# A two-layer RG-LRU and mLSTM trunk: a gate projection in seven half products, another product order, square roots in one block, and half of an output quarter moved

## The chip, the cores and the metric

The kernel runs as one program on one core of one Trainium2 chip. The metric is the device time of one execution in microseconds (us), the median of the runs shown. All matrix work is done by TensorE (PE in the profile, with its weight loads listed as PEld). VectorE (DVE), ScalarE (ACT) and GpSimd (POOL) do the rest, and SyncE (SP) issues the plain loads and stores.

## The reference

The input is x with 512 tokens of 1024 channels, in float32. Each of two layers computes, with h the modulated RMS norm of x:

```
u = h @ w_in[l]
rg_x, rg_z, ml_x, ml_o, ml_z = jnp.split(u, split_pts, axis=-1)
y_rg = rglru(causal_depthwise_conv(rg_x, ...), ...) * jax.nn.silu(rg_z)
y_ml = mlstm_branch(ml_x, ml_o, ...) * jax.nn.silu(ml_z)
y = jnp.concatenate([y_rg, y_ml], axis=-1) @ w_out[l]
x = x + gate[:, None, :] * y
```

Each of the five pieces of u has 1024 columns. The RG-LRU needs, of each channel, r = sigmoid(block product + bias), a power exp(-8 r softplus(-lambda)), a factor sqrt(1 - a*a), and a scan over the tokens. The mLSTM has four heads of 256 channels, worked in the quadratic form over four blocks of 128 tokens.

## The kernel before, in words

**Precision.** A float32 product is made of three: each operand is split into a high part (a cast to fp32r on ACT) and a low part (the difference, on DVE), and `mm3` (L505 to L508) issues high x high, high x low and low x high into the same PSUM bank. All matmuls are recorded by `Planner.mm` and so stand at L154. A weight unit is 512 KB: `load_raw` fetches it to a tile of kind raw, and `split` makes whi (L184, ACT) and wlo (L191, DVE), so each unit costs one pass on each of the two engines. There are six raw tiles, four whi and four wlo.

**Order.** Nothing is issued as it is written. The kernel records operations; `Planner.deadlines` places each by the due time of the matmul that needs it, from costs written into the class; `Planner.schedule` runs a list schedule over PE, ACT, DVE, POOL and SP; and `issue` emits the instructions in that order. Every engine then works through its own list in order, and waits where an operand isn't there.

**A layer.** The ml_x projection (tiles mx), the four heads' scores (p, v, S), then the gates ml_o and ml_z (`ml_oz`, tiles oz) head by head with the heads' value products between (num, yT). Then the RG part: the rg_x projection (`rg_x`) and the rg_z projection (`rg_z`), each in four groups g of 256 columns, the gate products (`rg_gates`, tiles pa and px), and `rg_tail` for channel blocks 0 to 3 (batch 0) and 4 to 7 (batch 1). Then the output product in three column ranges: 512 columns (`out_first`, tiles out), 256 columns (`out_quarter`, tiles outq), 256 columns block by block of tokens (`out_last`, tiles outq as well). Every range sums the mLSTM's 1024 rows first (the list `CORD`), then the RG-LRU's.

**A group** (`chan_group`, L764) has two weight units, one for each half of the 1024 input channels, and 48 matmuls: 2 column halves x 8 input blocks x 3, each with a 128x128 weight block stationary and all 512 tokens moving.

**Seven products.** `ml_oz` makes the 512 tokens x 1024 x 512 columns of a head's two gates from seven half-size products instead of eight: tokens, input channels and columns are each cut in two. Four combinations of the h blocks (`h_forms`, tiles sf, sh, sl) are made once per layer; the combinations of weight quarters are made in the raw tile, by an accumulating DMA that POOL issues (`qdma`, L241: raw<-raw). One tile, ta, goes through four forms in turn: it is split, added to, split again. A product is 24 matmuls with 256 columns moving. In `ml_oz` the products come in the order h11, s1, s2, h12, s3, h22, s4; the two input halves are the even and the odd blocks of 128 channels.

**rg_gates** clamps r's argument on DVE (`q<-pa,par`, L208) ahead of an Exp. **rg_tail** takes the four square roots of a batch (`om<-om`) as four separate operations, and ACT's functions need a table that holds them (ACT_TABLE_LOAD).

**Background.** The next modulation's products are summed on DVE between the rest (`mod_units`, tiles macc), two steps for each `step_mod`, and finished by matmuls (modT, gateps) in the output stage.

Of the kernel before, what the change touches and what calls it, by code (L numbers as in the profile page):

```python
# [19 lines left out]
L = 2  # L20
D = 1024
T = 512
NB = 4
# [23 lines left out]
class View:  # L47
# [21 lines left out]
    def spread(self, axis, n):  # L69
        shape = list(self.dummy.shape)  # L70
        shape.insert(axis, n)
        d = np.broadcast_to(np.expand_dims(self.dummy, axis), shape)
        return self._next(d, lambda a: a.unsqueeze(axis).to_broadcast(shape))

# [34 lines left out]
class Planner:  # L109
# [55 lines left out]
    def act(self, out, in_, func, scale=None, bias=None, accum=None, extra=0.0):  # L165
        def r(v):
            return v.ap() if isinstance(v, View) else v

        def emit():
            kw = {}  # L170
            if scale is not None:
                kw["scale"] = r(scale)
            if bias is not None:
                kw["bias"] = r(bias)
            if accum is not None:
                kw["accum_out"] = accum.ap()
            self.nc.scalar.activation(out=out.ap(), in_=in_.ap(), func=func, **kw)
# [3 lines left out]
        self.op("ACT", emit, outs, [in_, scale, bias], 0.1 + 0.00084 * in_.n + 0.093 * k + extra)  # L181

# [254 lines left out]
def trunk_kernel(ctx: ExitStack, tc: tile.TileContext, x, cT, params, bif, bgate, fg,  # L437
# [6 lines left out]
    def pools(name, n, **kw):  # L444
# [3 lines left out]
        "heap": pools("heap", 64),  # L448
# [139 lines left out]
    sp4, hb = keep("sp4", [128, L, 8]), keep("hb", [128, L, 16])  # L588

    def small_params():  # L590
# [8 lines left out]
        P.ts(hb, par[:, :, P_BA:P_BA + 16], 0.5, ALU.mult)  # L599

# [395 lines left out]
    def ml_oz(l, h, hT, st):  # L996
# [3 lines left out]
        src = w_oz[l, h].rearrange("u p (k w n) -> p u k w n", k=2, w=2)  # L1000
        q = [src[:, :, k, w, :] for k in range(2) for w in range(2)]
        form = [[(hT[2 * p + k][0][:, ts], hT[2 * p + k][1][:, ts]) for p in range(4)]
                for k, ts in ((0, slice(0, 256)), (1, slice(0, 256)), (1, slice(256, 512)))]
        h11, h12, h22 = form
# [5 lines left out]
        def quarter(src):  # L1010
            raw = P.tile("raw", (128, 4, 256), F32, "raw")
            P.dma(raw, src, 1 << 19)
            return raw

        def add(raw, src):
            P.qdma(raw, src, 1 << 19)
# [10 lines left out]
        def wide(name):  # L1027
            return slot(name, F32, (128, 2, 256))

        ta = quarter(q[0])  # L1030
        ps = product(h11, parts(ta))
        p1 = wide("ozp")
        P.acopy(p1, ps)
        tb = quarter(q[1])
        add(ta, tb)
        p5 = product(s1, parts(ta))
        c12, c22 = wide("ozc"), wide("ozc")
        P.acopy(c22, p5)
        td = quarter(q[3])
        add(ta, td)  # L1040
        ps = product(s2, parts(ta))
        u = wide("ozu")
        P.tt(u, ps, p1, ALU.add)
        P.tt(c12, c22, u, ALU.subtract)
        tc = quarter(q[2])
        ps = product(h12, parts(tc))
        o = [wide("oz") for _ in range(2)]
        z = [wide("oz") for _ in range(2)]
        P.tt(p1, ps, p1, ALU.add)
        P.act(o[0], p1, AF.Tanh, scale=0.5)  # L1050
        yield
        add(tb, td)
        ps = product(s3, parts(tb))
        P.tt(u, ps, u, ALU.add)
        P.tt(c22, c22, u, ALU.subtract)
        add(ta, tc)
        ps = product(h22, parts(ta))
        P.tt(u, ps, u, ALU.add)
        P.act(o[1], u, AF.Tanh, scale=0.5)
        ps = product(s4, parts(td))  # L1060
        P.tt(c12, ps, c12, ALU.add)
        for n, c in ((1, c22), (0, c12)):
            P.act(z[n], c, AF.Tanh, scale=0.5)
            P.stt(z[n], z[n], 1.0, c, ALU.add, ALU.mult)
# [75 lines left out]

    def rg_x(l, g, hT, st):
# [10 lines left out]
    def rg_gates(l, g, st):  # L1152
# [4 lines left out]
        for cc in range(2):  # L1157
# [9 lines left out]
            P.ts(q, pa, par[:, l, P_BA + r:P_BA + r + 1], ALU.add, 0.0, ALU.min)  # L1167
            P.act(tr, pa, AF.Tanh, scale=0.5, bias=hb[:, l, r:r + 1])
            P.act(q, q, AF.Exp)
# [12 lines left out]
    def rg_z(l, g, hT, st):  # L1182
        pz = chan_group(l, 4 + g, hT, ("rgz0", "rgz1"))
# [19 lines left out]
    def out_evac(l, ps, xt, cs):  # L1203

        cw = cs.stop - cs.start
        t = slot("og", F32, (128, cw))
        P.tt(t, ps, gate_t[l][:, cs], ALU.mult)
# [17 lines left out]

    def out_quarter(l, st, xt, side):
        y = st["y"]
        ps = [bank("outq", (128, 256)) for b in range(NB)]
        for u in range(4):
            wh, wl = load_w(w_out[l, 8 + u], (4, 256))  # L1230
            for b in range(NB):
                bs = slice(128 * b, 128 * b + 128)
                for k in range(4):
                    c = CORD[4 * u + k]
                    mm3(ps[b], y[c][0][:, bs], y[c][1][:, bs], wh[:, k, :], wl[:, k, :], u == 0 and k == 0,
                        u == 3 and k == 3)
            side(u)
        for b in range(NB):
            out_evac(l, ps[b], xt[b], slice(512, 768))

    def out_last(l, st, xt, units, b):
# [3 lines left out]
        for u, (wh, wl) in enumerate(units):  # L1245
            for k in range(4):
                c = CORD[4 * u + k]
                mm3(ps, y[c][0][:, bs], y[c][1][:, bs], wh[:, k, :], wl[:, k, :], u == 0 and k == 0, u == 3 and k == 3)
        out_evac(l, ps, xt[b], slice(768, 1024))
# [37 lines left out]
    for l in range(L):  # L1287
        st = {k: {} for k in ("xm", "xc", "S", "v", "oz", "sw", "y", "yt", "A", "xr", "ai", "rz", "gq", "gv")}
# [98 lines left out]
        rg_z(l, 3, hT, st)  # L1387
# [23 lines left out]
        units = [load_w(w_out[l, 12 + u], (4, 256)) for u in range(4)]  # L1411
# [85 lines left out]
```

## Time and profile before

| what | value |
|---|---|
| median of 3 runs | 827.79 us (827.75 to 828.91) |
| the profiled execution, its own time | 827.94 us |
| its span, first to last instruction | 826.0 us, so 1.9 us lie around the span |
| granted TensorE clock, mean | 0.999 |
| RG part of layer 0 on PE | 226.3 to 330.9 us |
| RG part of layer 1 on PE | 624.0 to 728.6 us |

Times inside the profile are us from the start of the span. A row of the chain of waits reads: start, length, engine, tile and line, and xN for so many instructions in a row. A row of the groups of instructions reads: line, engine, operation, out<-in, shapes, xcount | busy us, mean ns of one | idle time of the engine ahead of them. Matmuls overlap, so the mean length of one (280 or 390 ns) is not the distance from one to the next; the chain's pieces give that distance. On DVE and ACT as well an instruction starts a little before the one ahead of it has ended. A row of the windows holds, for each engine, busy us and the number of instructions, then the granted clock, the DMA share and GB/s.

### The profile page before, as it was taken

The page shows a single profiled execution, that of the slowest core. Times are in us where ns is not written, and L with a number is a line of the kernel's source. Part 1 is how long each engine was busy: PE and PEld are TensorE (multiplying, and loading weights), DVE is VectorE, ACT ScalarE, POOL GpSimd, SP SyncE. Part 2 cuts the span into 40 slices and gives each one's busy share as a digit, 9 for nine tenths or more (in the row PEclk, how much of TensorE's full clock was granted, in tenths as well). Part 3 has the DMA queues.
Part 4 walks back from the last instruction along what each step waited for, and adds up shares of the span by engine and source line. Part 5 has one row for each costly group of instructions (what it writes and reads, how often), then busy time and mean ns, then how long its engine had stood idle before and what let it go on. Part 6 is the DMA issues. An engine that isn't in the chain of part 4 may idle for free.

```text
span 826.0 us, 14051 instructions
## 1 busy us (share of the span) xinstructions
PE 807.3 (98%) x5222; PEld 718.8 (87%) x5222; DVE 676.5 (82%) x1339; ACT 536.2 (65%) x1049; POOL 66.0 (8%) x96
## 2 busy tenths in 40 slices
PE   4999999999999999999999999999999999999996
PEld 3778899999988888889999789999998888888996
DVE  4678976899999899989469886589999989995552
ACT  4468765687858979822148666648786797992221
POOL 3000012122100000000010001212210000000000
PEclk9999999999999999999999999999999999999999
DMA  8953255668533434787433434368753243483002
GB/s 302 336 216 111 71 126 131 126 155 203 154 102 127 154 112 161 253 293 263 181 99 102 150 92 87 52 160 198 182 130 124 102 157 104 150 312 120 26 1 102
DMA packets 53956, 124.46 MB, mean 151 GB/s; under 512 B 4865, under 2 KB 23297, under 8 KB 53889
## 3 DMA queue, kind: packets, MB, share of 16 engines
q1 hardware_dynamic: 49280, 106.80, 38.2%
q0 software_dynamic: 4608, 16.78, 11.5%
q8 instruction: 41, 0.67, 0.3%
q14 instruction: 27, 0.21, 0.1%
HBM read 102.58 MB, written 4.19 MB: 129 GB/s over the span
## 4 chain that ended last, share of the span: by engine, by line
PE 96%; ACT 1%; DMA 1%; DVE 1%; issue 0%; SPq 0%; POOLq 0%; ACTq 0%
PE oz L154 18%; PE mx L154 11%; PE outq L154 11%; PE rgx L154 11%; PE out L154 11%; PE rgz L154 11%; PE S L154 4%; PE num L154 3%; PE v L154 3%; PE p L154 3%; PE A L154 2%; PE px L154 1%; PE pa L154 1%; DMA x<-in_x_dram 1%; PE hT L163 1%; PE modps L154 1%
## 5 line engine op out<-in xcount | busy, mean ns | idle before, releaser
L184 ACT CAST whi<-raw 128x1024 fp32r<-128x1024 f32 (+1 forms) x157 | 156.4, 1003 | 112.1 <-PE out L154 32.5
L191 DVE TENSOR_TENSOR wlo<-raw,whi 128x1024 fp32r<-128x1024 f32 (+1 forms) x157 | 180.7, 1158 | 39.6 <-ACT whi L184 38.9
L154 PE MATMUL oz<-whi,sh 128*128 128x256 f32 x256 | 72.8, 284 | 0.0
L154 PE MATMUL oz<-whi,sl 128*128 128x256 f32 x256 | 72.3, 283 | 0.0
L154 PE MATMUL oz<-wlo,sh 128*128 128x256 f32 x256 | 72.1, 282 | 0.0
L154 PE MATMUL outq<-whi,yh 128*128 128x256 f32 x256 | 71.5, 283 | 0.0
L154 PE MATMUL outq<-whi,yl 128*128 128x256 f32 x256 | 71.3, 282 | 0.0
L154 PE MATMUL outq<-wlo,yh 128*128 128x256 f32 x256 | 71.2, 282 | 0.0
L154 PE MATMUL mx<-hh,whi 128*128 128x512 f32 (+1 forms) x166 | 59.5, 358 | 2.2 <-ACT whi L184 2.2
L154 PE MATMUL mx<-hl,whi 128*128 128x512 f32 (+1 forms) x166 | 58.1, 350 | 0.1
L154 PE MATMUL mx<-hh,wlo 128*128 128x512 f32 (+1 forms) x166 | 57.3, 348 | 0.0
L154 PE MATMUL oz<-wlo,hh 128*128 128x256 f32 x192 | 54.4, 284 | 0.0
L154 PE MATMUL oz<-whi,hh 128*128 128x256 f32 x192 | 54.2, 282 | 0.0
L154 PE MATMUL oz<-whi,hl 128*128 128x256 f32 x192 | 54.1, 282 | 0.0
L241 POOL DMA_DIRECT2D raw<-raw x32 | 27.7, 865 | 294.5 <-DVE wlo L191 127.8
L154 PE MATMUL rgx<-hh,whi 128*128 128x512 f32 x128 | 50.6, 395 | 0.0
L154 PE MATMUL rgz<-hh,wlo 128*128 128x512 f32 x128 | 50.5, 395 | 0.0
L154 PE MATMUL rgx<-hh,wlo 128*128 128x512 f32 x128 | 50.5, 394 | 0.0
L154 PE MATMUL out<-whi,yl 128*128 128x512 f32 x128 | 50.5, 394 | 0.0
L154 PE MATMUL out<-whi,yh 128*128 128x512 f32 x128 | 50.4, 394 | 0.0
L154 PE MATMUL rgx<-hl,whi 128*128 128x512 f32 x128 | 50.4, 393 | 0.0
L154 PE MATMUL rgz<-hh,whi 128*128 128x512 f32 x128 | 50.3, 393 | 0.0
(279 smaller groups left out, 2447.7 us busy)
## 6 DMA issues: line engine op xcount, KB each, us to landing
raw<-in_w_in_dram SPq DMA_DIRECT2D x45, 512.0 KB, 3.7
raw<-in_w_oz_dram SPq DMA_DIRECT2D x32, 512.0 KB, 5.0
raw<-raw POOLq DMA_DIRECT2D x32, 512.0 KB, 5.3
raw<-in_w_ada_dram SPq DMA_DIRECT2D x32, 512.0 KB, 4.4
raw<-in_w_out_dram SPq DMA_DIRECT2D x32, 512.0 KB, 3.6
wada<-in_w_adb_dram SPq DMA_DIRECT2D x24, 256.0 KB, 6.1
x<-in_x_dram SPq DMA_DIRECT2D x16, 256.0 KB, 5.8
raw<-in_w_qk_dram SPq DMA_DIRECT2D x8, 512.0 KB, 4.7
```

Source lines behind the costliest of these rows:

```text
L154: self.nc.tensor.matmul(out.ap(), lhsT=lhsT.ap(), rhs=rhs.ap(), start=start, stop=stop, **kw)
L163: self.op("PE", lambda: self.nc.tensor.transpose(out.ap(), in_.ap(), ident.ap()), [out], [in_, ident], 0.109)
L184: self.op("ACT", lambda: self.nc.scalar.copy(out.ap(), in_.ap()), [out], [in_], 0.1 + 0.00084 * in_.n)
L191: self.op(eng, lambda: e.tensor_tensor(out=out.ap(), in0=a.ap(), in1=b.ap(), op=op), [out], [a, b], c)
L241: self.op("POOL", lambda: self.nc.gpsimd.dma_start(out.ap(), in_.ap(), accum_op=ALU.add), [out], [out, in_], 1.3, tail=nbytes)
```

## The change: what it does, and the diff

- The seven products become a function of their own, `seven`, in the order h11, h12, s1, s4, then s2, s3, h22. `ml_oz` uses it, and so does `chan_pair`, a new projection of two groups at once with the weights stationary and 256 tokens moving. The input halves are now blocks 0 to 3 and 4 to 7, in `h_forms` too, and a quarter of the oz weights comes in two loads of 256 KB.
- `rg_z` of groups 0 and 1 is made by `chan_pair` (its columns 4 and 5), in two parts: four products, then, after the gates of group 1 and `rg_x` of group 2, three. Groups 2 and 3 keep the old form (`rg_z1`).
- The four square roots of a batch are one operation of the planner (`sqrts`).
- The clamp in `rg_gates` goes to ACT as a Relu with a negated bias (`nba`), and the sign into the Exp's scale.
- `out_ml` makes the mLSTM rows' share of the columns 512 to 767 (two of the four weight units of `out_quarter`) between `rg_z1` of group 2 and the gates of group 3, and copies it to SBUF (tiles oml). `out_quarter` then makes the other two units and adds the copy. The planner's heap has 65 slots instead of 64.

```diff
-        a, b = hv.pop(2 * p), hv.pop(2 * p + 1)
+        a, b = hv.pop(p), hv.pop(p + 4)
...
+    def seven(hT, st, quarter, product, out):
...
+        ta = quarter(0, 0)
+        ps = product(h11, parts(ta))
+        p1 = wide("sp")
+        P.acopy(p1, ps)
+        tb = quarter(0, 1)
+        P.qdma(ta, tb, 1 << 19)
+        tc = quarter(1, 0)
+        out((0, 0), product(h12, parts(tc)), p1)
+        td = quarter(1, 1)
+        ps = product(s1, parts(ta))
+        c22, c12 = wide("sc"), wide("sc")
+        P.acopy(c22, ps)
+        P.qdma(ta, td, 1 << 19)
+        ps = product(s4, parts(td))
+        P.tt(c12, ps, c22, ALU.add)
+        yield
+        P.qdma(tb, td, 1 << 19)
+        ps = product(s2, parts(ta))
+        P.tt(p1, ps, p1, ALU.add)
+        P.tt(c12, c12, p1, ALU.subtract)
+        out((0, 1), None, c12)
+        P.qdma(ta, tc, 1 << 19)
+        ps = product(s3, parts(tb))
+        P.tt(p1, ps, p1, ALU.add)
+        P.tt(c22, c22, p1, ALU.subtract)
+        out((1, 1), None, c22)
+        out((1, 0), product(h22, parts(ta)), p1)
...
+            raw = P.tile("raw", (128, 2, 2, 256), F32, "raw")
+            for u in range(2):
+                P.dma(raw[:, u], src[:, 2 * k + u, :, w, :], 1 << 18)
...
+    def chan_pair(l, g, hT, st, name):
...
+            return load_raw(w_in[l, g + w, k], (4, 256))
...
+                for k in range(4):
+                    mm3(ps[:, cc, :], w[0][:, k, cs], w[1][:, k, cs], f[k][0], f[k][1],
+                        cc == 0 and k == 0, cc == 1 and k == 3)
...
+        for dst, c in dst22:
+            P.acopy(dst, c)
...
-            P.ts(q, pa, par[:, l, P_BA + r:P_BA + r + 1], ALU.add, 0.0, ALU.min)
+            P.act(q, pa, AF.Relu, scale=-1.0, bias=nba[:, l, r:r + 1])
...
-        for n in range(4):
-            P.act(om[n], om[n], AF.Sqrt, extra=0.7)
+        P.sqrts(om)
...
+        if part is not None:
+            P.tt(part, ps, part, ALU.add)
...
+    def out_ml(l, q, st):
...
+        for u in range(2):
+            wh, wl = load_w(w_out[l, 8 + 4 * q + u], (4, 256))
...
+            P.acopy(t, ps[n])
...
-        rg_z(l, 0, hT, st)
-        step_mod(bg, 2)
+        rgz = rg_z(l, 0, hT, st)
+        next(rgz)
         rg_gates(l, 1, st)
-        rg_z(l, 1, hT, st)
-        step_mod(bg, 2)
+        rg_x(l, 2, hT, st)
+        next(rgz)
         rg_tail(l, 0, st)
-        rg_x(l, 2, hT, st)
         rg_x(l, 3, hT, st)
         rg_gates(l, 2, st)
-        rg_z(l, 2, hT, st)
+        rg_z1(l, 2, hT, st)
+        step_mod(bg, 2)
+        out_ml(l, 0, st)
         step_mod(bg, 2)
         rg_gates(l, 3, st)
-        rg_z(l, 3, hT, st)
+        step_mod(bg, 2)
+        rg_z1(l, 3, hT, st)
```

Three places show what that makes of the instruction lists. The first is PE in layer 0 where the first rg_z product follows the gate products of group 0 (px); hh and hl are the high and low parts of h. Before:

```order
L154 MATMUL px_3830<-xrl_3750,whi_3571 128x512
L154 MATMUL px_3830<-xrh_3734,wlo_3709 128x512
L154 MATMUL rgz0_3838<-hh0_676,whi_3621 128x512
L154 MATMUL rgz0_3838<-hl0_680,whi_3621 128x512
L154 MATMUL rgz0_3838<-hh0_676,wlo_3760 128x512
L154 MATMUL rgz0_3838<-hh1_786,whi_3621 128x512
```

And now, at the same place:

```order
L158 MATMUL px_3844<-xrl_3783,whi_3633 128x512
L158 MATMUL px_3844<-xrh_3774,wlo_3743 128x512
L158 MATMUL rgz_3852<-hh0_681,whi_3586 128x256
L158 MATMUL rgz_3852<-hl0_685,whi_3586 128x256
L158 MATMUL rgz_3852<-hh0_681,wlo_3635 128x256
L158 MATMUL rgz_3852<-hh1_793,whi_3586 128x256
```

Each matmul moves 256 columns instead of 512. In the whole list 192 of the 384 rg_z matmuls with 512 columns are gone and 336 with 256 have come: 96 less and 168 more in each layer. The oz matmuls are as many as before.

The second place is PE at the end of rg_z of group 2 (rgz1). Before, the gate products of group 3 (pa, px) follow:

```order
L154 MATMUL rgz1_4321<-hl7_1119,whi_4206 128x512
L154 MATMUL rgz1_4321<-hh7_1112,wlo_4230 128x512
L154 MATMUL pa_4394<-xrh_4314,whi_4122 128x512
L154 MATMUL pa_4394<-xrl_4329,whi_4122 128x512
L154 MATMUL pa_4394<-xrh_4314,wlo_4134 128x512
```

Now the moved half of the output quarter stands between, with the mLSTM's result as its stationary operand (yh, yl):

```order
L158 MATMUL rgz1_4393<-hl7_1118,whi_4319 128x512
L158 MATMUL rgz1_4393<-hh7_1111,wlo_4331 128x512
L158 MATMUL outq_4472<-whi_4334,yh_2808 128x256
L158 MATMUL outq_4472<-wlo_4353,yh_2808 128x256
L158 MATMUL outq_4472<-whi_4334,yl_2884 128x256
```

There are 96 such rows before pa of group 3 comes, and 96 fewer in `out_quarter`.

The third place is DVE ahead of the operands of the gate products of group 2 (xrl is the low part of the convolved rg_x; rows of L224 and, in the changed kernel, L236 are the scans). Before, batch 0's scans and products with the gate (ti<-q,ti and ti<-ti,rzt) stand among them:

```order
L224 SCALAR_TENSOR_TENSOR ti_3962<-q_3960,ti_3962 128x512
L224 SCALAR_TENSOR_TENSOR ti_3991<-q_3979,ti_3991 128x512
L199 SCALAR_TENSOR_TENSOR rconv_4148<-rxf_4140,par_430,rconv_4148 128x511
L191 TENSOR_TENSOR ti_3858<-ti_3858,rzt_3946 128x512
L199 SCALAR_TENSOR_TENSOR rconv_4148<-rxf_4140,par_430,rconv_4148 128x510
L191 TENSOR_TENSOR wlo_4177<-raw_3981,whi_4160 128x1024
L199 SCALAR_TENSOR_TENSOR rconv_4179<-rxf_4168,par_430,rconv_4179 128x511
L199 SCALAR_TENSOR_TENSOR rconv_4148<-rxf_4140,par_430,rconv_4148 128x509
L199 SCALAR_TENSOR_TENSOR rconv_4179<-rxf_4168,par_430,rconv_4179 128x510
L191 TENSOR_TENSOR ti_3962<-ti_3962,rzt_4084 128x512
L199 SCALAR_TENSOR_TENSOR rconv_4179<-rxf_4168,par_430,rconv_4179 128x509
L191 TENSOR_TENSOR xrl_4211<-rconv_4148,xrh_4198 128x512
```

Now the same operands come among the sums of the seven products (sp, sc, rgz), and batch 0's first products of the tail only after them:

```order
L211 SCALAR_TENSOR_TENSOR rconv_4205<-rxf_4191,par_433,rconv_4205 128x510
L203 TENSOR_TENSOR wlo_4253<-raw_4001,whi_4216 128x1024
L211 SCALAR_TENSOR_TENSOR rconv_4205<-rxf_4191,par_433,rconv_4205 128x509
L211 SCALAR_TENSOR_TENSOR om_4236<-om_4236,tr_4086 128x512
L203 TENSOR_TENSOR xrl_4276<-rconv_4180,xrh_4250 128x512
L203 TENSOR_TENSOR sp_3924<-rgz_4163,sp_3924 128x512
L203 TENSOR_TENSOR xrl_4289<-rconv_4205,xrh_4272 128x512
L203 TENSOR_TENSOR rgz_3943<-rgz_4201,sp_3924 128x256
L203 TENSOR_TENSOR rgz_3952<-rgz_4201,sp_3924 128x256
L203 TENSOR_TENSOR wlo_4299<-raw_4056,whi_4243 128x1024
L203 TENSOR_TENSOR sc_3983<-sc_3983,sp_3924 128x512
L203 TENSOR_TENSOR ti_3854<-ti_3854,om_4060 128x512
```

The work of batch 0's tail has gone behind the operands of group 2.

Of the other lists: POOL has 40 accumulating DMAs instead of 32 (four more in each layer, for rg_z), SP has 64 loads of oz weights instead of 32 of twice the size, DVE and ACT have six more splits of weight units, and ACT has 8 table loads instead of 17.

More of the change, by code (lines that the diff above doesn't have):

```diff
@@ L181, in act, with sqrts, emit @@
         self.op("ACT", emit, outs, [in_, scale, bias], 0.1 + 0.00084 * in_.n + 0.093 * k + extra)
+    def sqrts(self, tiles):
+        def emit():
+            for t in tiles:
+                self.nc.scalar.activation(out=t.ap(), in_=t.ap(), func=AF.Sqrt)
+        self.op("ACT", emit, tiles, tiles, 2.6 + sum(0.1 + 0.00084 * t.n for t in tiles))
     def acopy(self, out, in_):
@@ L588, in trunk_kernel @@
     sp4, hb = keep("sp4", [128, L, 8]), keep("hb", [128, L, 16])
+    nba = keep("nba", [128, L, 8])
     def small_params():
@@ L599, in small_params @@
         P.ts(hb, par[:, :, P_BA:P_BA + 16], 0.5, ALU.mult)
+        P.ts(nba, par[:, :, P_BA:P_BA + 8], -1.0, ALU.mult)
     gs_t, sh_t, gate_t, mod_acc = {}, {}, {}, {}
@@ L994, in gate_chain @@
         yield
[L996 to L1004, printed above, removed]
+    def seven(hT, st, quarter, product, out):
+        h11, h12, h22 = [[(hT[4 * k + p][0][:, ts], hT[4 * k + p][1][:, ts]) for p in range(4)]
+                         for k, ts in ((0, slice(0, 256)), (1, slice(0, 256)), (1, slice(256, 512)))]
         s1, s2, s3, s4 = [[st["sf"][p][n] for p in range(4)] for n in range(4)]
@@ L1025, in product, with out @@
             return ps
[L1027 to L1062, printed above, removed]
+        o = [slot("oz", F32, (128, 2, 256)) for _ in range(2)]
+        z = [slot("oz", F32, (128, 2, 256)) for _ in range(2)]
+        def out(name, ps, c):
+            n, w = name
+            if ps is not None:
+                P.tt(o[n], ps, c, ALU.add)
+                c = o[n]
+            if w == 0:
+                P.act(o[n], c, AF.Tanh, scale=0.5)
+            else:
+                late.append((n, c))
+        late = []
+        yield from seven(hT, st, quarter, product, out)
+        for n, c in late:
             P.act(z[n], c, AF.Tanh, scale=0.5)
@@ L1139, in ml_yt, with quarter, product, out @@
             st["y"][8 + 2 * h + dc] = (hi, lo)
+    def chan_pair(l, g, hT, st, name):
+        res = [slot(name) for _ in range(4)]
+        def quarter(k, w):
+            return load_raw(w_in[l, g + w, k], (4, 256))
+        def product(f, w):
+            ps = bank(name, (128, 2, 256))
+            for cc in range(2):
+                cs = slice(128 * cc, 128 * cc + 128)
+                for k in range(4):
+                    mm3(ps[:, cc, :], w[0][:, k, cs], w[1][:, k, cs], f[k][0], f[k][1],
+                        cc == 0 and k == 0, cc == 1 and k == 3)
+            return ps
+        def out(at, ps, c):
+            n, w = at
+            for cc in range(2):
+                dst = res[2 * w + cc][:, 256 * n:256 * n + 256]
+                if ps is not None:
+                    P.tt(dst, ps[:, cc, :], c[:, cc, :], ALU.add)
+                else:
+                    dst22.append((dst, c[:, cc, :]))
+        dst22 = []
+        for _ in seven(hT, st, quarter, product, out):
+            yield
+        for dst, c in dst22:
+            P.acopy(dst, c)
+        yield res
     def rg_x(l, g, hT, st):
@@ L1182, in rg_z, with rg_z1 @@
     def rg_z(l, g, hT, st):
+        steps = chan_pair(l, 4 + g, hT, st, "rgz")
+        yield next(steps)
+        for cc, pz in enumerate(next(steps)):
+            st["rz"][2 * g + cc] = silu2(pz, "rz")
+        yield
+    def rg_z1(l, g, hT, st):
         pz = chan_group(l, 4 + g, hT, ("rgz0", "rgz1"))
@@ L1228, in out_quarter @@
         ps = [bank("outq", (128, 256)) for b in range(NB)]
-        for u in range(4):
+        us = range(2, 4) if (0, 0) in st["oml"] else range(4)
+        for u in us:
             wh, wl = load_w(w_out[l, 8 + u], (4, 256))
@@ L1244, in out_last @@
         bs = slice(128 * b, 128 * b + 128)
[L1245 removed]
+        for u, (wh, wl) in units:
             for k in range(4):
                 c = CORD[4 * u + k]
[L1248 to L1249 removed]
+                mm3(ps, y[c][0][:, bs], y[c][1][:, bs], wh[:, k, :], wl[:, k, :], u == units[0][0] and k == 0,
+                    u == 3 and k == 3)
+        out_evac(l, ps, xt[b], slice(768, 1024), st["oml"].get((1, b)))
     def final_pre(xt):
@@ L1410, in trunk_kernel @@
             pre = [final_pre(xt[b]) for b in range(NB)]
-        units = [load_w(w_out[l, 12 + u], (4, 256)) for u in range(4)]
+        units = [(u, load_w(w_out[l, 12 + u], (4, 256))) for u in (range(2, 4) if (1, 0) in st["oml"] else range(4))]
         for b in range(NB):
```

41 lines of the change are left out of this document (28 added, 13 removed).

## The prediction

> **What bounds the kernel now.** I began with the page's busy times and the line of shares of the chain that ended last.
>
> ```profile
> PE 807.3 (98%) x5222; PEld 718.8 (87%) x5222; DVE 676.5 (82%) x1339; ACT 536.2 (65%) x1049; POOL 66.0 (8%) x96
> PE 96%; ACT 1%; DMA 1%; DVE 1%; issue 0%; SPq 0%; POOLq 0%; ACTq 0%
> ```
>
> PE is busy for 98% of the span and carries 96% of the chain. Next I asked what PE itself waited for, by total, times and longest wait.
>
> ```profile
> PE modps L154 <- DMA wada<-in_w_ada_dram: 9.4, 2, 8.1
> PE mx L154 <- ACT whi L184: 2.2, 1, 2.2
> PE cumb L154 <- DVE lf L199: 0.2, 1, 0.2
> ```
>
> These are all its waits in the list, 11.8 us, and the two large ones (modps, and the first mx) belong to the start, which the change leaves as it is but for one small DVE row. From then on the time is the sum of the distances between matmuls. So the question is how many columns PE streams less, and whether the other engines still deliver ahead of it.
>
> **The change part by part.** The terms on PE come from the chain's pieces: start, length, what, and how many matmuls in a row.
>
> ```profile
> 168.86 7.46 PE oz L154 x63
> 255.80 11.13 PE rgz L154 x48
> 269.71 11.12 PE rgz L154 x48
> 376.38 16.97 PE outq L154 x144
> 434.79 17.01 PE mx L154 x144
> 653.47 11.12 PE rgz L154 x48
> 667.37 11.11 PE rgz L154 x48
> ```
>
> *The rg_z products.* The four groups that change (0 and 1 of each layer) take 11.13 + 11.12 + 11.12 + 11.11 = 44.48 us now, 0.232 us for each of 192 matmuls with 512 columns. The new form has 336 with 256 columns. The mx row is the very same form, a weight block stationary and 256 tokens of h moving: 17.01 / 144 = 0.1181 us; the oz row gives 7.46 / 63 = 0.1184. So the new products take 336 x 0.1181 = 39.7 us, by the oz row 39.8. The term is 39.7 - 44.5 = -4.8 us, with the end at -4.7. It is smaller than an eighth of 44.5 (5.6) because two matmuls of 256 cost 0.236 and one of 512 costs 0.232. Nothing hides this work, since PE waits for nobody there.
>
> A rule speaks against halving the width: the Trainium skill (TensorE: Matmul & The Clock Gate, Back-to-back issue gap) gives about 131 ns for sustained load-and-multiply pairs at 512 columns and about 81 ns at 128. By a straight line between them, an estimate, 256 would take 98 ns, and the term would be 336 x 0.098 - 192 x 0.131 = +7.8 us. The trace disagrees, with 232 and 118 ns, so the sum goes by the rows.
>
> *The moved half of the output quarter.* 96 matmuls with 256 columns leave `out_quarter` and come before the gates of group 3: by the outq row 96 x 16.97 / 144 = 11.3 us in each layer, moved and not added. It puts 11.3 us of PE work between the RG operands and the first use of batch 1's result.
>
> *The oz products* are as many as before, in another order, and the h blocks' pairing costs nothing on PE. The sum on PE is -4.8 us.
>
> Now the engines beside it. Their rows, with mean ns of one:
>
> ```profile
> L191 DVE TENSOR_TENSOR wlo<-raw,whi 128x1024 fp32r<-128x1024 f32 x145 | 176.1, 1219 | 39.6 <-ACT whi L184 38.9
> L224 DVE TENSOR_TENSOR_SCAN ti<-q,ti 128x512 f32<-128x512 f32 x16 | 19.3, 1215 | 0.1
> L208 DVE TENSOR_SCALAR q<-pa,par 128x512 f32<-128x512 f32 x16 | 12.0, 747 | 0.0
> L191 DVE TENSOR_TENSOR ti<-ti,rzt 128x512 f32<-128x512 f32 x16 | 10.8, 685 | 0.0
> L191 DVE TENSOR_TENSOR ozc<-ozc,ozu 128x512 f32<-128x512 f32 x16 | 10.9, 683 | 0.0
> L191 DVE TENSOR_TENSOR og<-outq,gate 128x256 f32<-128x256 f32 x16 | 6.7, 422 | 20.5 <-PE outq L154 20.5
> L184 ACT CAST whi<-raw 128x1024 fp32r<-128x1024 f32 x145 | 152.4, 1052 | 112.1 <-PE out L154 32.5 <-PE oz L154 22.1 <-PE outq L154 15.7
> L177 ACT ACT_TABLE_LOAD x17 | 21.8, 1283 | 1.1 <-PEq L1486 0.8
> L177 ACT ACTIVATE tr<-pa,hb 128x512 f32<-128x512 f32 x16 | 10.8, 688 | 0.0
> L184 ACT COPY ozc<-oz 128x512 f32<-128x512 f32 x8 | 4.7, 584 | 1.9 <-DVE vl L191 0.9 <-PE num L154 0.9
> L184 ACT COPY vf<-v 128x256 f32<-128x256 f32 x32 | 11.1, 381 | 5.1 <-PE v L154 2.5 <-DVE xml L191 2.2
> ```
>
> DVE in one layer: three more splits (seven forms for four units), 3 x 1.219 = 3.7; the sums of the seven products, five like ozc and four like og, 5 x 0.683 + 4 x 0.422 = 5.1; the clamps gone, 8 x 0.747 = -6.0; the added half in `out_quarter`, 4 x 0.422 = 1.7. That is +4.5, of which +2.8 stand in the RG part, and the two splits of the moved units, 2.4, move there too. ACT in one layer: three splits 3.2, eight Relus taken like tr<-pa,hb 5.5, four copies of whole products 2.3, four half-wide ones 1.5, and in all layers together nine table loads less, -11.5. That is +12.5 - 5.8 = +6.7 a layer. All of it is covered by PE's matmuls as long as the operands come early. What the cover is worth shows in the windows (PE, PEld, DVE, ACT and POOL busy us, then clock, DMA share, GB/s) and in three pairs of an operand's end and its first use. The windows first, one of the oz part and two of the RG part:
>
> ```profile
> 168.86:176.32 7.46, 7.46 (x65) 7.46 (x64) 6.94 (x23) 5.52 (x16) 1.66 (x3) 1.00 1.02 222
> 288.00:308.00 20.00, 20.00 (x88) 16.17 (x87) 20.00 (x28) 14.83 (x22) 0.00 (x0) 1.00 0.32 106
> 308.00:328.00 20.00, 20.00 (x88) 16.18 (x87) 20.00 (x30) 18.88 (x31) 0.00 (x0) 1.00 0.43 141
> ```
>
> Then three rows of DVE in order of time (start, length):
>
> ```profile
> 181.43 1.23 DVE L191 TENSOR_TENSOR wlo<-raw,whi 128x1024 fp32r<-128x1024 f32 x1
> 299.92 0.69 DVE L191 TENSOR_TENSOR xrl<-rconv,xrh 128x512 fp32r<-128x512 f32 x1
> 320.88 1.23 DVE L191 TENSOR_TENSOR wlo<-raw,whi 128x1024 fp32r<-128x1024 f32 x1
> ```
>
> And the three of PE that use what these made:
>
> ```profile
> 183.30 0.28 PE L154 MATMUL oz<-wlo,hh 128*128 128x256 f32 x1
> 303.14 0.39 PE L154 MATMUL pa<-xrl,whi 128*128 128x512 f32 x1
> 330.98 0.40 PE L154 MATMUL out<-wlo,yh 128*128 128x512 f32 x1
> ```
>
> By the two lists, each DVE row feeds the PE row in the same place. So an oz weight was ready 0.6 us ahead (182.66 to 183.30), the gate operand of group 2 2.5 us ahead (300.61 to 303.14), and the first output weight 8.9 us ahead (322.11 to 330.98). DVE is full in the RG part. But the changed list puts batch 0's tail behind group 2's operands: four scans and eight products, 4 x 1.215 + 8 x 0.685 = 10.3 us of DVE, against the 2.8 that came; so that lead of 2.5 grows. From there PE gets 11.3 us more and DVE 2.4. I take no wait there, with 0 to 2 us in each layer as the bounds.
>
> *The accumulating chain.* POOL's rows, from the view of its raw<-raw issues (the issue's length in ns as min/median/max, and the landing):
>
> ```profile
> L241 POOL DMA_DIRECT2D raw<-raw x32: 841/854/1043, 106.3 to 607.2; - x32
> DMA to landing us min/median/max: 4.5/5.3/9.2
> ```
>
> One link, from one split of ta to the next, is 5.3 + 1.05 (whi) + 1.22 (wlo) = 7.6 us, and three links join h11 to h22: 22.8 us. In the old order five products lie between their first matmuls, 120 x 0.118 = 14.2 us, in the new one six, 17.0. The chain may start 2.8 us later in a head than it had to before, so the new order asks for less. In rg_z, six products, 12 gate matmuls and 48 of rg_x lie between: 17.0 + 60 x 0.232 = 30.9 us, more than the 22.8 it needs. The four more issues in a layer (0.85 us each) find POOL idle: the windows from 288 us on show it at 0.00. SP's 32 more issues have no one behind them that waits for less than a landing, and I cost them at nothing; if the two halves of a quarter land later, that is the rival below.
>
> *The start* gets one more DVE row (nba, 16 columns), bounded by the smallest and a usual row at 0 to 0.2 us; the square roots in one block shorten ACT. The block does wait for the last of its four inputs, and behind it on ACT stand copies of rg_x and casts of weights; ACT has room for such a wait where it is at 14.83 and 18.88 of 20 us, and the leads above are what a late cast would use up first. On POOL the first addition of rg_z stands ahead of the power operations (mrs) of the last head's norm, whose result PE's transposes (yT) take before the first gate products; that addition only needs the first split of ta, which DVE's list has ahead of the last head's norm, so I cost it at nothing, and at its 0.85 us if it comes late.
>
> The sum against the profiled execution: 827.9 - 4.8 + 0.1 = 823.2 us. The median of the runs lies 0.15 below that execution, so I forecast 823.0. A difference of 0.2% (1.7 us) is about what a measurement of this kernel can tell from no change.
>
> **The rivals.**
>
> *The forecast:* PE stays dense, 821.5 to 825 with small waits either way. For it speak the waits, of which none lie in the parts that change, and leads that grow where DVE is fullest.
>
> *The gain goes into new waits in the RG part.* DVE was at 20.00 of 20 us there. If group 2's operands or the weights of rg_z come 2 to 3 us late in each layer, the 2.4 us saved per layer are given back: 827.9 - 4.8 + 5 = 828. It decides where DVE's own list falls behind the 2.5 us of the pair above. Against it stand the 10.3 us that left that place. If DVE alone set the part, it would be 827.9 + 2 x 2.8 = 833.5, but the lead of 8.9 us at the output would have to be used up first.
>
> *Slower, by the oz chain.* The mechanism is the accumulation behind each head's last product: h22 now waits for the third addition with two products, 5.7 us, between s2 and itself, where it had three (8.5), and half as large loads of twice the number share the DMA engines, whose share was already 1.02 in the oz window above. With 2.8 us spare over three links the price starts when a landing takes 5.3 + 0.9 = 6.2 us. At 6.6, a third of the way to the largest one seen (9.2), a chain is 3.9 longer, 1.1 beyond the spare, and 8 heads give 8.8: 823.2 + 8.8 = 832. For it speaks the lead of 0.6 us; against it that the bytes are the same and the sum of the links got easier. The Trainium skill (SBUF, Who interferes with whom) says that DVE instructions with two SBUF inputs contend with GpSimd instructions that read SBUF, and (SBUF: two separate sides) that GpSimd can be kept from writing the descriptors of its DMAs; the trace has 5.3 us as the median although DVE was busy 6.94 of 7.46 us there, so it shows no such starving so far.
>
> *Slower, by width.* If a 256-wide matmul took more than 44.48 / 336 = 0.132 us here, the half products would lose; at 0.155 they cost 7.6 us, and the time is 835.5. The skill's rule above points that way; the mx, oz and outq rows at 0.118 leave it next to nothing.
>
> That the change doesn't do what it says is excluded by PE's list, which has the 336 and lacks the 192.
>
> **How the numbers follow.** Forecast 0.80; gain eaten in the RG part 0.10; oz chain 0.08; width 0.02. Faster by over 0.2% is the first case, 0.80; within it the second, 0.10; slower the last two, 0.10. The time is the likeliest case's, 823.0. The range runs from 821.5, 1.5 below, a margin that I chose for gaps between unlike matmuls, which these rows don't price, to 827.0, where waits of 2 us in each layer have taken most of the gain; outside lie most of the second case and the last two.
>
> **What would show it.** In the profile of the changed kernel: rgz pieces of 96 and 72 matmuls in 11.3 and 8.5 us; no row of PE waiting for whi, wlo, xrl or raw after the start; PE busy about 802 of 821 us; ACT_TABLE_LOAD x8; DVE near 685 us. I am wrong if PE's waits name wlo or whi at oz or rgz, if the landing of raw<-raw moves above 6 us, or if the pieces of rgz take more than 0.12 us for a matmul.

## The result, and the profile after

| what | before | after |
|---|---|---|
| median | 828.11 us (4 runs) | 823.26 us (4 runs) |
| ratio of the two, 95% interval | | 0.9942, 0.9930 to 0.9953 |
| span of the profiled execution | 826.0 us | 821.5 us |

The forecast was 823.0. The page of the changed kernel, its busy times and the shares of the chain that ended last:

```profile
PE 802.7 (98%) x5366; PEld 722.1 (88%) x5366; DVE 684.2 (83%) x1356; ACT 544.4 (66%) x1078; POOL 76.8 (9%) x104
PE 94%; DVE 1%; ACT 1%; issue 1%; DMA 1%; SPq 1%; POOL 0%; ACTq 0%; DVEq 0%; POOLq 0%
```

PE is busy 4.6 us less in a span that is 4.5 us shorter, so its idle time is what it was. Its waits (total us, times, longest) are still those of the kernel before:

```profile
PE modps L158 <- DMA wada<-in_w_ada_dram: 9.3, 2, 8.0
PE mx L158 <- ACT whi L196: 2.2, 1, 2.2
PE cumb L158 <- DVE lf L211: 0.3, 1, 0.3
```

The four new pieces of the chain (start, length, what, how many) hold the gain:

```profile
256.04 11.32 PE rgz L158 x96
281.26 8.52 PE rgz L158 x72
651.40 11.37 PE rgz L158 x96
676.71 8.52 PE rgz L158 x72
```

The four sum to 39.73 us, where 44.48 stood: 4.75 less. 39.73 / 336 is 0.1182 us for a matmul.

The other engines: the groups of table loads, then two rows of the view of POOL's raw<-raw issues.

```profile
L181 ACT ACT_TABLE_LOAD x4 | 5.1, 1283 | 0.9 <-PEq L1573 0.8
L191 ACT ACT_TABLE_LOAD x4 | 5.1, 1283 | 0.1
```

```profile
L253 POOL DMA_DIRECT2D raw<-raw x40: 841/857/1046, 112.1 to 665.7; - x40
DMA to landing us min/median/max: 4.5/4.9/7.3
```

There are 8 table loads now, where there were 17. The 40 accumulating additions land in 4.9 us in the median, sooner than the 5.3 of before, and none later than 7.3. Last, the pair of group 2 on which the RG rival rested, the end of xrl on DVE and its first use on PE:

```profile
293.38 0.69 DVE L203 TENSOR_TENSOR xrl<-rconv,xrh 128x512 fp32r<-128x512 f32 x1
```

```profile
300.98 0.39 PE L158 MATMUL pa<-xrl,whi 128*128 128x512 f32 x1
```

The lead there was 2.5 us and is now 300.98 - 294.07 = 6.9.

### The profile page after: what moved, and what is told of

Its sections match the earlier page's. It is cut to its first block, busy times and chain, and to the rows that moved or that the text cites. A ratio compares the mean times of both kernels' runs of the same rounds, so it can differ in the third digit from the quotient of the medians.

```text
span 821.5 us, 14567 instructions
## 1 busy us (share of the span) xinstructions
PE 802.7 (98%) x5366; PEld 722.1 (88%) x5366; DVE 684.2 (83%) x1356; ACT 544.4 (66%) x1078; POOL 76.8 (9%) x104
## 4 chain that ended last, share of the span: by engine, by line
PE 94%; DVE 1%; ACT 1%; issue 1%; DMA 1%; SPq 1%; POOL 0%; ACTq 0%; DVEq 0%; POOLq 0%
PE oz L158 19%; PE rgx L158 11%; PE out L158 11%; PE mx L158 11%; PE rgz L158 10%; PE outq L158 10%; PE S L158 4%; PE num L158 3%; PE v L158 3%; PE p L158 3%; PE A L158 2%; PE pa L158 1%; PE px L158 1%; PE modps L158 1%; PE yT L167 1%
## 5 line engine op out<-in xcount | busy, mean ns | idle before, releaser
L196 ACT CAST whi<-raw 128x1024 fp32r<-128x1024 f32 (+1 forms) x163 | 162.3, 1004 | 108.7 <-DMA raw<-in_w_out_dram 27.4
L203 DVE TENSOR_TENSOR wlo<-raw,whi 128x1024 fp32r<-128x1024 f32 (+1 forms) x163 | 187.3, 1159 | 32.5 <-ACT whi L196 32.4
L253 POOL DMA_DIRECT2D raw<-raw x40 | 34.7, 866 | 342.2 <-DVE wlo L203 151.0
L158 PE MATMUL out<-wlo,yh 128*128 128x512 f32 x128 | 50.4, 394 | 0.0
L158 PEld LDWEIGHTS oz<-whi,sh 128*128 128x128 f32 x256 | 48.2, 188 | 0.7 <-ACT sp L196 0.6
```

The lines of the kernel that those rows point to most:

```text
L158: self.nc.tensor.matmul(out.ap(), lhsT=lhsT.ap(), rhs=rhs.ap(), start=start, stop=stop, **kw)
L196: self.op("ACT", lambda: self.nc.scalar.copy(out.ap(), in_.ap()), [out], [in_], 0.1 + 0.00084 * in_.n)
L203: self.op(eng, lambda: e.tensor_tensor(out=out.ap(), in0=a.ap(), in1=b.ap(), op=op), [out], [a, b], c)
L253: self.op("POOL", lambda: self.nc.gpsimd.dma_start(out.ap(), in_.ap(), accum_op=ALU.add), [out], [out, in_], 1.3, tail=nbytes)
```

## The experiments

All are edits of the changed kernel. Their ratios are against the kernel before, measured beside each of them on the same chip; the changed kernel's own is 0.9942.

### The whole products back: rgz_full

```diff
-        rgz = rg_z(l, 0, hT, st)
-        next(rgz)
+        rg_z1(l, 0, hT, st)
...
-        next(rgz)
+        rg_z1(l, 1, hT, st)
```

> The changed kernel with the rg_z of groups 0 and 1 back as whole 512-wide products (96 matmuls in each layer instead of 168 half-wide ones); the oz order, the pairing, the Relu, the block of square roots and the moved half stay. Theory (the gain is the sum of the distances between rg_z's matmuls): 192 x 0.232 - 336 x 0.118 = +4.8 us against the changed kernel, so 828.1, level with the kernel before (ratio 1.000), and PE without a wait after the start. Rival (the other edits carry a part of the gain, by leads that grew or by fewer table loads): clearly under 828, some 825 to 827, ratio 0.997 to 0.999.

Measured: 829.22 us, ratio 1.0012 (1.0004 to 1.0021). Without the half products nothing of the gain is left; the other edits alone cost about 1 us. One of the pieces of 48 matmuls that stand here in place of those of 96 and 72:

```profile
281.42 11.13 PE rgz L158 x48
```

PE's waits were those of the kernel before, so that 1 us is no wait. It is spread over small differences in the distances between matmuls, the largest at num (0.7) and mx (0.5), and I could not place it further. The rival, that the other edits carry a part of the gain, falls.

### The seven products alone: rgz_alone

```diff
-        yield from seven(hT, st, quarter, product, out)
+        yield from seven_oz(hT, st, quarter, product, out)
...
-            P.act(q, pa, AF.Relu, scale=-1.0, bias=nba[:, l, r:r + 1])
+            P.ts(q, pa, par[:, l, P_BA + r:P_BA + r + 1], ALU.add, 0.0, ALU.min)
...
-        P.sqrts(om)
+        for n in range(4):
+            P.act(om[n], om[n], AF.Sqrt, extra=0.7)
...
-        out_ml(l, 0, st)
```

(`seven_oz` issues the old order.)

> The changed kernel with all but the seven half products of rg_z undone: old product order in oz (its quarters still loaded in two halves, and the new pairing of the blocks), clamps on DVE instead of Relu on ACT, four separate square roots, all 24 units of the output quarter behind the tail. Theory: the gain of 4.8 us stays where no operand comes late; DVE gets its 6.0 us a layer of clamps back in the RG part, where the smallest lead of the changed kernel is 5 to 7 us for the gates, so 823.3 with 0 to 2 us of waits, ratio 0.994 to 0.997. Rival (DVE sets the RG part; the other edits are what pays for the seven products there): PE waits for xrl, wlo or yl in each layer, 2 to 6 us in all, 825.5 to 829, ratio 0.997 to 1.001.

Measured: 832.76 us, ratio 1.0055 (1.0038 to 1.0072): slower than the kernel before, and slower than the rival's 825.5 to 829. The rival's place of the wait was right. PE's list of waits has a new row:

```profile
PE out L158 <- DVE wlo L203: 5.3, 2, 2.7
```

In order of time, DVE ahead of that wait, and PE at it:

```profile
359.10 2.73 DVE L211 SCALAR_TENSOR_TENSOR macc<-raw,csil,macc 128x512 f32<-128x512 f32 x4
361.76 2.48 DVE L211 SCALAR_TENSOR_TENSOR yl<-ti,yh 128x512 fp32r<-128x512 f32 x4
364.16 1.21 DVE L203 TENSOR_TENSOR wlo<-raw,whi 128x1024 fp32r<-128x1024 f32 x1
```

```profile
362.37 0.40 PE L158 MATMUL out<-whi,yh 128*128 128x512 f32 x1
365.43 0.79 PE L158 MATMUL out<-wlo,yh 128*128 128x512 f32 x1 [2.66 <-DVE wlo L203]
366.88 0.63 PE L158 MATMUL out<-wlo,yh 128*128 128x512 f32 x1
367.30 0.63 PE L158 MATMUL out<-whi,yl 128*128 128x512 f32 x1
```

By the two lists, the late weight is not the first unit of the output's first range but its seventh, the one that DVE splits behind the tail's last yl. And the wait costs more than its 2.66 us: behind it the matmuls stand 0.43 us apart (366.88 to 367.30) and not 0.23. The windows around it (PE, PEld, DVE, ACT, POOL busy us, granted clock, DMA share, GB/s) show a lower clock there:

```profile
348.00:362.70 14.70, 14.70 (x64) 11.64 (x62) 14.70 (x20) 6.16 (x9) 0.00 (x0) 1.00 0.32 105
362.70:365.40 2.70, 0.07 (x1) 0.00 (x0) 2.70 (x5) 0.00 (x0) 0.00 (x0) 0.87 0.83 258
365.40:371.50 6.10, 6.07 (x14) 4.78 (x15) 6.10 (x10) 1.04 (x1) 0.00 (x0) 0.50 0.79 282
```

DVE is full ahead of the wait, and for 6.1 us behind it the granted clock is 0.50. The span is 832.8 - 821.5 = 11.3 us longer than the changed kernel's. The distances between the out matmuls hold 10.3 of it: 5.7 at the two waits, one in each layer, and 4.7 at the 24 matmuls right behind them, most of which stand 0.43 us apart. The last 1.0 us stayed unplaced.

The profiled execution is the slowest of six, 834.56 us at a mean clock of 0.992. The quickest took 829.38 us at 0.998, a clock like the changed kernel's (0.997 to 0.999), and is 6.1 us above that kernel's median, about the waits' own length. A stretch of 6.1 us at 0.50 takes 0.004 off the mean clock, an estimate, so the clock can hardly have fallen there as it did here.

The Trainium skill (TensorE: Matmul & The Clock Gate, HAM oscillation) says that the clock is halved by gaps of over about 3.4 us. The trace agrees in kind, with 0.50 granted, but a gap of 2.66 us was enough in this execution.

### Which of the companions was needed: half_back, clamp_back, oz_back

Each undoes one part of what rgz_alone had undone together: the call of `out_ml` deleted; the clamp and the four square roots; the old order in oz.

> The changed kernel with only the moved half undone: all units of the output quarter are again multiplied behind the tail, and 11.3 us of PE work in each layer no longer stand between the gates of groups 2 and 3. Theory (the moved half is the cover that lets DVE finish the operands of the first output units): the first out weights, some 8 us ahead in the changed kernel, lose 11.3 us of cover and win back two splits, 2.4, so they come some 0.5 to 1.5 us late in each layer; with matmuls that run at half the clock behind such a wait, as in the run before (2.7 us of wait cost 5), 825 to 828. Rival (the clamps on DVE made the wait in the run with the seven products alone): no wait here, 823.3.

Measured: 824.65 us, ratio 0.9954 (0.9942 to 0.9966), and no wait of PE over 0.3 us behind the start.

> The changed kernel with only the clamps back on DVE in place of Relu on ACT, and the square roots one by one again. Theory (the moved half is the cover): DVE gets 6 us a layer more, half of it ahead of the first out weights that are some 8 us early, so they still come in time; 823.3, ratio to the kernel before 0.994 to 0.996. Rival (the clamps made the wait): PE waits for wlo at out, up to 2.7 us in each layer, 827 to 833.

Measured: 824.01 us, ratio 0.9949 (0.9937 to 0.9961), and again none over 0.3 us.

> The changed kernel with only the old order of the seven products in oz (loads in two halves and new pairing kept). Theory (the chain of additions fitted in either order, and the new one only widens the leads): the smallest lead of an oz weight shrinks from 0.7 to about 0.4 us and PE still waits for none; 823.3, ratio 0.994 to 0.996. Rival (the new order pays): PE waits for wlo at oz at some heads, 824.5 to 828.

Measured: 824.68 us, ratio 0.9956 (0.9943 to 0.9969); the new waits, one at oz among them, are of 0.2 us.

All three intervals overlap the changed kernel's and none has the wait, so no single one of these edits makes it, and neither theory of a single culprit holds. The leads of the seventh output unit show the main part. In the changed kernel, the end of its split on DVE and its first use on PE:

```profile
365.62 1.22 DVE L203 TENSOR_TENSOR wlo<-raw,whi 128x1024 fp32r<-128x1024 f32 x1
```

```profile
373.46 0.40 PE L158 MATMUL out<-wlo,yh 128*128 128x512 f32 x1
```

And the same two with the moved half back behind the tail:

```profile
360.26 1.22 DVE L203 TENSOR_TENSOR wlo<-raw,whi 128x1024 fp32r<-128x1024 f32 x1
```

```profile
362.30 0.40 PE L158 MATMUL out<-wlo,yh 128*128 128x512 f32 x1
```

With the clamps and the separate square roots back, but the moved half in place:

```profile
365.53 1.22 DVE L203 TENSOR_TENSOR wlo<-raw,whi 128x1024 fp32r<-128x1024 f32 x1
```

```profile
374.06 0.39 PE L158 MATMUL out<-wlo,yh 128*128 128x512 f32 x1
```

The lead is 373.46 - 366.84 = 6.6 us with the moved half, 362.30 - 361.48 = 0.8 without it, and 374.06 - 366.75 = 7.3 in clamp_back. So the moved half is what covers this unit: without it the lead is almost used up, though nothing waits yet. The clamps and the square roots alone take nothing from it. From 0.8 us ahead to 2.66 late it takes one more of the edits undone in rgz_alone (the clamps, the square roots, the old oz order); which one is not shown, since no run undid the moved half together with just one of them.

### Seven products for groups 2 and 3 as well: rgz_all, rgz_all_room, rgz_layer2

```diff
-        rg_z1(l, 2, hT, st)
+        rgz = rg_z(l, 2, hT, st)
+        next(rgz)
...
-        rg_z1(l, 3, hT, st)
+        next(rgz)
```

> The changed kernel with the rg_z of groups 2 and 3 in seven half products too. Theory (sum of distances): another 192 x 0.232 - 336 x 0.118 = -4.8 us, 818.4 and ratio 0.988 against the kernel before, if the leads of 5 to 7 us in the RG part cover three more splits (3 x 1.22) and the sums of the products (5 x 0.68 + 4 x 0.42) of DVE, 8.8 us in each layer less the evacuations that they replace. Rival (DVE is full there, so that the gain is eaten): PE waits for wlo, xrl or yl, up to 2 x (8.8 - 5) = 7.6 us, 818.4 + 2 to 7.6 = 820 to 826.

Measured: 848.87 us, ratio 1.0250 (1.0237 to 1.0263), far above the theory and the rival. The waits are there and many; the largest new ones:

```profile
PE pa L158 <- ACT xrh L196: 5.3, 4, 1.8
PE outq L158 <- DVE wlo L203: 4.9, 2, 2.5
PE modT L158 <- DVE macc L211: 3.0, 1, 3.0
PE out L158 <- DVE wlo L203: 2.7, 2, 1.7
```

But DVE is not full ahead of the first of them. The window before it, and ACT's own waits in the 16 us around it:

```profile
295.00:307.00 12.00, 12.00 (x76) 10.75 (x75) 5.14 (x7) 5.68 (x8) 1.70 (x2) 1.00 0.47 111
```

```profile
ACT whi L196 <- PE rgx L158: 6.5, 2, 4.6
ACT rxf L196 <- DVE ti L211: 1.3, 1, 1.3
```

DVE is busy for 5.14 and ACT for 5.68 of 12 us; ACT's next casts wait until rgx matmuls have ended. The h combinations live on to the end of the RG part here, 16 tiles of the heap. So the next run gave it room: four more heap tiles, two result tiles less for a pair of groups, and no copies of the sums of groups 1 and 3, which the tail takes where they lie.

```diff
-        "heap": pools("heap", 65),
-        "raw": pools("raw", 6),
+        "heap": pools("heap", 69),
+        "raw": pools("raw", 5),
...
-        res = [slot(name) for _ in range(4)]
+        res = [slot(name) for _ in range(2)]
...
+        z = [silu2(c, "rz", (128, 2, 256)) for c in late]
+        for cc in range(2):
+            st["rz"][2 * g + 2 + cc] = [(slice(256 * n, 256 * n + 256), z[n][:, cc]) for n in range(2)]
...
-MODAT = ({(0, 2): 6, (1, 0): 10, (1, 1): 11}, {(1, 2): 6})
+MODAT = ({(0, 2): 6, (1, 0): 11, (1, 1): 12}, {(1, 2): 6})
```

> The rg_z of groups 2 and 3 in seven half products too, as in the slow run of that kind, but with more room: 69 heap tiles instead of 65 (one raw buffer of six given up for them), the sums of groups 1 and 3 taken to the tail where they lie, in half tiles, without the copies, and the two sums for the next layer's modulation a unit later. Theory (that run was slow because its tiles found no room, so operands were made late): with the room PE stays dense and the gain of another 4.8 us shows, 818.5, ratio 0.988 to 0.990. Rival (DVE has no time left in the RG part, whatever the room: 150 of 165 us busy there and 8.8 more): PE waits for xrl, wlo or yl at gates and out, 822 to 840.

Measured: 824.31 us, ratio 0.9952 (0.9935 to 0.9969): 24.6 us better with the same matmuls. The waits at the gates, where DVE and ACT had been half idle, are gone, so there a full engine was not what rgz_all suffered from. That it was the tiles is argued and not shown apart: the heap, the result tiles and the copies changed together, and the modulation's sums came later in the same run, so a part of the 3.0 us at modT may be theirs. The waits that stayed:

```profile
PE out L158 <- DVE wlo L203: 3.4, 2, 2.1
PE outq L158 <- DVE wlo L203: 1.3, 1, 1.3
PE modT L158 <- DVE macc L211: 1.1, 1, 1.1
```

In this execution, the slowest of seven (821.96 to 826.69 us), they make 5.8 us, more than the 4.8 that the products save. Three of the four are in the first layer, where the modulation's macc work also lies on DVE. So the last run of this series keeps the second layer's pair alone, with the same room, and covers its output as the change had done:

```diff
+        if l == 1:
+            rgz = rg_z(l, 2, hT, st)
+            next(rgz)
+        else:
+            rg_z1(l, 2, hT, st)
...
+        if l == 1:
+            out_ml(l, 1, st)
         rg_tail(l, 1, st)
```

> The changed kernel with the rg_z of groups 2 and 3 in seven half products in the second layer alone, with the 69 heap tiles and five raw buffers of the run with room, the sums of groups 1 and 3 taken to the tail where they lie, and in that layer the other mLSTM half of the output columns moved ahead of the tail as well, as a cover for the output's first weights; the modulation's sums at their old places. Theory (with tiles and cover PE stays dense): one pair of groups saves 2.4 us, 823.3 - 2.4 = 820.9, ratio 0.991 to 0.992. Rival (DVE has no time left there either): PE waits for wlo at out in the second layer, as the 2.1 us of the run with room, and 822.5 to 826.

Measured: 819.50 us, ratio 0.9896 (0.9882 to 0.9910): faster than both kernels. PE has no wait over 0.3 us behind the start, and the pieces of the second layer's groups 2 and 3 are

```profile
696.76 11.34 PE rgz L158 x96
722.18 8.52 PE rgz L158 x72
```

19.86 us in place of 11.14 + 11.13. The span is 3.8 us shorter than the changed kernel's; 2.4 of it are these, the other 1.4 are small differences in num and v that I did not place. Whether the room or the cover was what this run needed is not shown, as both came together.

### A narrower matmul: w128

```diff
-        pz = chan_group(l, 4 + g, hT, ("rgz0", "rgz1"))
+                    for t in range(4):
+                        chan_mm(pz[cc], u, hT, kh, k, cc, slice(128 * t, 128 * t + 128),
```

> The changed kernel with each 512-wide matmul of rg_z in groups 2 and 3 issued as four of 128 columns (768 instead of 192 in all; the computation is the same). What a narrow matmul costs. Theory (the distance follows the columns, as from 0.232 to 0.118): 0.059 us each, a piece of 192 in 11.4 us instead of 11.1, +1 us in all, 824.2. Rival (there is a floor for a matmul with its own weight load): by the 128-wide yT rows of the trace, 0.87 us for 8, the floor is 0.109 us, a piece takes 20.9 us and the kernel 823.3 + 4 x 9.8 = 862. The Trainium skill (TensorE: Matmul & The Clock Gate, Back-to-back issue gap) gives about 81 ns for a pair at 128 columns: by it a piece would take 15.6 us and the kernel 841.

Measured: 865.50 us, ratio 1.0453 (1.0439 to 1.0466), with PE dense. A piece of the chain:

```profile
304.39 21.39 PE rgz L158 x192
```

21.39 / 192 = 0.111 us: 128 columns cost all but what 256 cost, 0.118. So there is a floor, at the clock of 1.00 that the windows show there, and the half products stand close above it. The Trainium skill's 81 ns for a pair at 128 columns (TensorE: Matmul & The Clock Gate, Back-to-back issue gap) is not reached here. Whether the floor is one of the weight load or of the fp32r type the run does not tell.

### A longer chain of additions in oz: hold_new, hold_old, hold_long

```diff
+        def emit():
+            if hold:
+                self.nc.gpsimd.memset(out[:, 0:3].ap(), 0.0)
+            self.nc.gpsimd.dma_start(out.ap(), in_.ap(), accum_op=ALU.add)
```

> The changed kernel with each link of oz's chain of additions made longer: ahead of each addition, POOL clears three quarters of the block that it is added to (so three quarters of the oz weights are not the right ones from the second product on). By the POOL rows of clearing 256 and 512 columns, 0.31 and 0.68 us, 768 take some 1.05 us, an estimate; three links come 3.2 us later. Theory (the new order leaves 2.8 us more than the old one between the ends of the chain, and the leads of the oz weights start at 0.7 us): 3.2 fits into 3.5, so 823.3 to 826, PE with small waits at oz or none. Rival (the chain is as tight in the new order as in the old): 2.5 us late at each of 8 heads, 843 and more.

Measured: 824.70 us, ratio 0.9957 (0.9943 to 0.9970), within the theory's range. The clearing took 0.74 us, not 1.05.

> The same longer links in the changed kernel with the old order of oz's products (again three quarters of the oz weights are not the right ones from the second product on). Theory: the leads there are 0.4 to 0.6 us, so three links that come 3.2 us later make PE wait some 2.6 us at each of 8 heads, 21 us, and with matmuls at half the clock behind such a wait up to as much again: 845 to 865. Rival (the chain can start earlier, or the order makes no difference): within 2 us of the same kernel with short links, 824.7 to 827.

Measured: 824.42 us, ratio 0.9955 (0.9942 to 0.9967), against 0.9956 with short links. The theory falls: 3 x 0.74 = 2.2 us more in the chain did nothing in the old order either, where the leads are down to 0.4 us and less. So those leads are not set by the chain. The last run made the links 2.2 us longer each:

> The changed kernel with each link of oz's chain longer by three clearings of 768 columns, 3 x 0.74 = 2.2 us by the rows of the run with one (again those oz weights are not the right ones). By the prediction's arithmetic (three links against the distance of the matmuls): 3 x 2.2 - 2.8 - 0.7 = 3.1 us late at each of 8 heads, 25 us, 848 and, with matmuls at half the clock behind the waits, more. Rival (the additions have room of their own: in the changed kernel the second and the third of a head are issued 13.9 to 15.3 us apart, and a link needs 7.2): a link of 9.4 us fits there, and only the first one, issued 8.5 to 10.8 us ahead of the second, can be up to 1 us short: 823.5 to 832.

Measured: 825.80 us, ratio 0.9975 (0.9966 to 0.9984), some 2.7 us above the changed kernel and not 25. Its rows of POOL and of PE's waits:

```profile
L255 POOL MEMSET raw<- 128x768 f32 x96 | 73.9, 770 | 220.5 <-DVE wlo L203 187.5 <-DMA raw<-raw 20.8 <-DVE den L227 8.4
```

```profile
PE cumb L167 <- DVE mrow L236: 1.0, 1, 1.0
PE yT L167 <- DVE tmp L211: 0.6, 2, 0.3
```

PE waits for no oz weight even here; 1.6 us of the 2.7 are these two rows. The timeline of POOL in the kernel before, which the prediction did not read, shows the room (one head's four additions):

```profile
160.19 0.84 POOL L241 DMA_DIRECT2D raw<-raw  x1 [1.49 <-DVE wlo L191]
...
168.07 0.85 POOL L241 DMA_DIRECT2D raw<-raw  x1 [3.14 <-DMA raw<-in_w_oz_dram]
173.27 0.84 POOL L241 DMA_DIRECT2D raw<-raw  x1 [4.34 <-DVE wlo L191]
...
184.35 0.90 POOL L241 DMA_DIRECT2D raw<-raw  x1 [7.13 <-DVE dg L199]
```

And the first matmul of that head's h11 on PE:

```profile
176.39 0.28 PE L154 MATMUL oz<-whi,hh 128*128 128x256 f32 x1
```

By POOL's list the first, third and fourth of these additions go to ta, and the second to tb. Those to ta stand 13.1 and 11.1 us apart where a link needs 7.6, so 5.5 and 3.5 us are to spare, and the first is issued 16.2 us ahead of h11's first matmul. In the changed kernel the additions to ta of a head are at the least 10.3 us apart, so that a link of 9.4 fits there too. The expectation above took the second addition for one to ta; its 8.5 to 10.8 us are the distance to an addition of tb, and no link was short.

## Why the prediction was right, and where it was not

- **The sum on PE** was right, in the term and in its size. Forecast -4.8, measured -4.75 by the pieces; 0.1182 us a matmul against 0.1181. rgz_full confirms it from the other side, with about 1 us more than the pieces explain.
- **The width** was weighed rightly: 256 columns at 0.118. Towards still narrower matmuls there is nothing left to win: w128 shows the floor at 0.111.
- **The RG part.** No wait came, as forecast, and the lead of 2.5 us grew to 6.9. But the pairs that I watched were not the tightest. The prediction counted the moved half as cover ("From there PE gets 11.3 us more and DVE 2.4") and looked at the output's first weight, 8.9 us ahead; the smallest lead is the seventh's, 6.6 us with the moved half and 0.8 without. "I take no wait there" held, and by half_back would have held without the moved half as well, but by 0.8 us only; with the moved half, the Relu, the joined square roots and the new oz order all undone, the same products are slower than the kernel before.
- **The rival of new waits** was priced too low: 2 to 3 us late in each layer were to give back the gain, "827.9 - 4.8 + 5 = 828". In rgz_alone 2.66 us late in each layer made 11.3 in the profiled execution, against 6.1 in the quickest. The step that failed is that a wait costs its own length alone; the slower matmuls behind the two waits, 4.7 us where the clock fell, were missing.
- **The oz chain** failed in one step, "three links join h11 to h22: 22.8 us", set against 14.2 us of matmuls. The chain does not start with h11's matmuls: in the head shown its first addition is issued 16.2 us ahead of them, and the additions are 24.2 us apart from first to last. The spare was not 2.8 us, and the price did not start at a landing of 6.2: 2.2 us more in every link cost 2.7 us in all, with no wait for an oz weight. The lead of 0.6 us that was to speak for this rival was read off a weight outside the chain: by the lists it is h12's, the quarter tc, which takes no addition.
- **DVE and ACT.** DVE was to come near 685 and has 684.2. ACT's busy time rose by 8.2 us, not 13.4: I added lengths of instructions, and those did rise by some 14 us; the page counts stretches in which two overlap once. Nothing hung on it.

## What to carry to other kernels

When PE is dense, a change to its instruction stream is worth the difference of the measured distances, and the forecast's work lies in the cover: find for each stage the operand with the smallest lead and not the first one, and see which edits of the same change feed it. Price a wait of PE of over 2 us at its own length at the least, and at up to twice that where the clock falls behind it. If an edit that should gain makes many waits with DVE and ACT half idle ahead of them, look for tiles that are held too long before blaming an engine.

## What the runs showed of the hardware that I had not expected

- In the profiled execution of rgz_alone the granted clock fell to 0.50 behind a wait of PE of 2.66 us, and stayed there for 6.1 us. In another execution of that kernel the mean clock was 0.998, so not every such wait brings the fall. Shorter waits went either way: in rgz_all_room the clock stayed at 1.00 behind one of 1.3 us (at 370 us), and was 0.71 behind the second of two that came within 6 us (at 400 and 405 us):

```profile
369.90:371.30 1.40, 0.11 (x2) 0.04 (x1) 1.40 (x3) 1.04 (x1) 0.00 (x0) 1.00 0.85 298
371.30:378.00 6.70, 6.70 (x29) 5.47 (x30) 6.70 (x11) 1.06 (x1) 0.00 (x0) 1.00 0.82 282
405.30:406.50 1.20, 0.05 (x2) 0.03 (x1) 1.20 (x3) 0.00 (x0) 0.00 (x0) 1.00 0.78 300
406.50:412.00 5.50, 5.50 (x35) 5.50 (x36) 5.50 (x13) 2.04 (x7) 0.00 (x0) 0.71 0.88 273
```

- At a granted clock of 1.00, a matmul of 128 columns with its own weights cost 0.111 us, one of 256 columns 0.118, one of 512 columns 0.232.
